# A hybrid diffusion step on one core: instruction order from the scheduler's timeline model

## The chip, the cores and the metric

The kernel runs on one core of a Trainium2 chip. A core has TensorE (PE, matmuls; PEld is its weight load), VectorE (DVE), ScalarE (ACT), GpSimd (POOL) and SyncE (SP), each with an instruction queue of its own that is worked off in order, and 16 DMA engines. The metric is the time of one execution on the device in microseconds (us), the median of several runs.

## The reference, cut to what matters

One inference step of a two-layer backbone of width 1024 over 640 tokens (128 context tokens, 512 latent tokens on a grid 64 wide). Layer 0 mixes tokens by a gated DeltaNet in both directions, layer 1 by neighbourhood attention; each mixer is followed by a gated ConvFFN of width 2816. Norms are RMSNorms with adaLN: shift, scale and gate are linear in SiLU of a conditioning vector (`modulation`).

```python
def modulation(cvec, w, b):
    m = jax.nn.silu(cvec) @ w + b
    return [t[:, None, :] for t in jnp.split(m, N_MOD, axis=-1)]
...
for l in range(DEPTH):
    mods, cmods = modulation(c, w_ada[l], b_ada[l]), modulation(c_ctx, ...)
    x = x + gate1 * mixer_l(rmsnorm(x) * (1 + scale1) + shift1)      # DeltaNet, then attention
    h = rmsnorm(x) * (1 + scale2) + shift2
    u = dwconv(h @ w_up)                 # two halves: value and gate
    x = x + gate2 * ((silu(u_gate) * u_value) @ w_down)
y = rmsnorm(x)
```

The block above is a condensed paraphrase below `modulation`. DeltaNet works in chunks of 64 tokens: for each head and direction a triangular inverse per chunk, and then a scan over the chunks in which the state S of one chunk enters the next.

## The kernel before, in words

Everything is held transposed: 128 channels on the partitions, the 640 tokens along the free axis, as eight tiles of the width. A product of f32 precision is made of three matmuls in a 32-bit reduced format: the weights are split into a high part `wh…` (a ScalarE cast, L373) and a low part `wl…` (a VectorE subtraction, L375), the activations into `hh` and `hl` (L346), and `pass3` (L385, L386, L387) issues high·high, high·low and low·high. So each weight tile has a DMA into a staging tile `wst…`, a cast on ScalarE and a subtraction on VectorE ahead of its matmuls.

Stages in the order of the program: adaLN products and the projections of the DeltaNet, its chunk work and scans (names `kk`, `p…` for chunk products, `sb`, `S`, `osb` in the scan, L915 to L972), its out-projection (`rgo`), the norm, FFN 0, the attention (heads in pairs `0` to `7`, names `s`, `t`, `no` on TensorE, `Ps`, `ptw` on VectorE; its out-projection is issued in an early part `rne` and a late part `rno`), the norm, FFN 1, the final norm.

An FFN takes 22 tiles of the hidden width. For each it makes two products, `duv` and `dug` (up-projection, value and gate halves, two halves of the tokens one after the other), in PSUM buffers of the pool `pd` (two; the pool `pa` has three smaller ones); a depthwise convolution of each follows (`conv`: ScalarE writes the middle tap at L437, VectorE adds the outer taps at L442 into `yv` and `yg`), then the gated product into `F`. The 22 tiles are worked in three groups; behind each, the down-projection `rdn` accumulates over the group's tiles of `F`, for eight output tiles (`rdn000` to `rdn007` for layer 0, group 0), and VectorE adds each to the residual stream `X` (L451).

The adaLN vectors that are needed only later are not made on TensorE but on VectorE: `ada_rows` loads rows of `w_ada` (256 KB tiles `adr…`) and reduces each with the conditioning vector, for both of its versions (`cb`, two reductions of 128 x 512 per tile, `adj` and `adr` as their throw-away outputs, L250). In FFN 0 `between` draws one or two steps of this generator behind each hidden tile, in FFN 1 another set in the same way.

The Python code doesn't give the order on the engines directly. The program is recorded by the tile framework, whose list scheduler then picks, engine by engine, which ready instruction is next. `behind` / `issue_after` (L320 to L328) forbid it to put certain instructions ahead of a given one, and `high_priority` raises some. Apart from these and from data dependences, the order follows from the scheduler's estimate of when an instruction would be ready and how long it takes.

## Time and profile before

| | |
|---|---|
| median of 3 runs | 1908.26 us (1902.61 to 1912.27) |
| profiled execution | 1907.08 us |
| its span, first to last instruction | 1905.1 us |
| granted TensorE clock, mean | 0.976 |
| busy: PE, PEld | 1808.2, 1717.7 us |
| busy: DVE, ACT, POOL | 1277.3, 724.3, 261.1 us |
| DMA | 194.15 MB, 102 GB/s mean |

All times of the trace are us from the start of the span of this one execution. The profile lists busy time by engine, the span in forty slices with the busy share of each engine in tenths, groups of equal instructions, waits with what ended them, and windows (a stretch, its length, then busy time and number of instructions of PE, PEld, DVE, ACT and POOL, the granted clock, the DMA share and GB/s). In the trace the DeltaNet's chunk work and scans run from about 100 to 560, FFN 0 from about 617 to 1084, the attention to about 1387, FFN 1 from about 1436 to the end.

### The profile page before, as it was taken

What the parts mean: (1) busy time and instruction counts of PE and PEld (TensorE: products, weight loads), DVE (VectorE), ACT (ScalarE), POOL (GpSimd) and SP (SyncE); (2) the same over time, 40 slices, a digit from 0 to 9 for tenths busy, and PEclk for the clock granted to TensorE, in tenths of its full rate; (3) what the DMA queues carried; (4) which work ended last, traced back from release to release, by engine and by line L of the source; (5) the groups of instructions that cost most, each with busy time, mean ns of one, the idle gap of its engine ahead of it and who ended that gap; (6) DMA issues with size and microseconds to landing.
All of it is one profiled execution on the core that took longest, in us unless ns stands there. A gap on an engine that the chain in (4) does not pass through costs nothing.

```text
span 1905.1 us, 34317 instructions
## 1 busy us (share of the span) xinstructions
PE 1808.2 (95%) x13587; PEld 1717.7 (90%) x13587; DVE 1277.3 (67%) x3100; ACT 724.3 (38%) x1456; POOL 261.1 (14%) x317
## 2 busy tenths in 40 slices
PE   6889899999879999999999999999999999999998
PEld 5878788887869999999999988888899999999998
DVE  6788658768666999855366689545679743653564
ACT  4553344343443342233144344444453421421443
POOL 1332123121202112110000211111131000000000
PEclk9989899999889999999999999999999999999999
DMA  7223123322222455542223254222233312222231
GB/s 293 74 81 106 39 103 114 93 64 80 74 97 93 143 169 160 160 159 67 82 83 111 71 164 153 76 74 71 68 122 117 117 56 78 88 71 75 88 90 56
DMA packets 102480, 194.15 MB, mean 102 GB/s; under 512 B 39496, under 2 KB 59034, under 8 KB 99560
## 3 DMA queue, kind: packets, MB, share of 16 engines
q1 hardware_dynamic: 94528, 165.50, 27.6%
q0 software_dynamic: 7248, 25.94, 4.3%
q8 instruction: 107, 1.75, 0.4%
q10 hardware_dynamic: 544, 0.52, 0.1%
q14 instruction: 53, 0.43, 0.1%
HBM read 183.09 MB, written 12.46 MB: 103 GB/s over the span
## 4 chain that ended last, share of the span: by engine, by line
PE 48%; DVE 4%; issue 2%; DMA 2%; ACT 1%; POOL 0%; DVEq 0%; POOLq 0%; ACTq 0%
PE duv L385 4%; PE duv L386 4%; PE dug L385 4%; PE dug L386 4%; PE duv L387 4%; PE dug L387 4%; PE rdn L385 4%; PE rdn L386 4%; PE rdn L387 4%; DMA bias<-cols 1%; PE dvn L385 1%; PE dvn L386 1%; PE dvn L387 1%; PE dqn L385 1%; PE no L1323 1%
## 5 line engine op out<-in xcount | busy, mean ns | idle before, releaser
L385 PE MATMUL duv<-hh,whuv 128*128 128x256 f32 (+1 forms) x704 | 215.8, 306 | 6.1 <-DVE yv L442 6.1
L385 PE MATMUL rdn<-F,whdn 128*128 128x384 f32 (+1 forms) x704 | 216.1, 307 | 3.1 <-DVE X L451 3.1
L386 PE MATMUL rdn<-F,whdn 128*128 128x384 f32 (+1 forms) x704 | 215.5, 306 | 0.0
L387 PE MATMUL rdn<-F,wldn 128*128 128x384 f32 (+1 forms) x704 | 215.5, 306 | 0.0
L385 PE MATMUL dug<-hh,whug 128*128 128x256 f32 (+1 forms) x704 | 215.2, 306 | 0.2 <-DVE yg L442 0.2
L386 PE MATMUL duv<-hl,whuv 128*128 128x256 f32 (+1 forms) x704 | 215.2, 306 | 0.0
L387 PE MATMUL duv<-hh,wluv 128*128 128x256 f32 (+1 forms) x704 | 215.2, 306 | 0.0
L386 PE MATMUL dug<-hl,whug 128*128 128x256 f32 (+1 forms) x704 | 215.2, 306 | 0.0
L387 PE MATMUL dug<-hh,wlug 128*128 128x256 f32 (+1 forms) x704 | 215.1, 306 | 0.0
L385 PEld LDWEIGHTS duv<-hh,whuv 128*128 128x128 f32 x704 | 132.2, 188 | 6.6 <-ACT whug L373 3.8
L385 PEld LDWEIGHTS rdn<-F,whdn 128*128 128x128 f32 x704 | 132.4, 188 | 3.8 <-issue 1.9
L451 DVE SCALAR_TENSOR_TENSOR X<-rdn,mods,X 128x128 f32<-128x128 f32 (+1 forms) x144 | 54.9, 433 | 116.0 <-PE rdn L387 115.9
L385 PEld LDWEIGHTS dug<-hh,whug 128*128 128x128 f32 x704 | 132.1, 188 | 0.3 <-issue 0.3
L387 PEld LDWEIGHTS duv<-hh,wluv 128*128 128x128 f32 x704 | 132.2, 188 | 0.1
L387 PEld LDWEIGHTS dug<-hh,wlug 128*128 128x128 f32 x704 | 132.2, 188 | 0.0
L386 PEld LDWEIGHTS duv<-hl,whuv 128*128 128x128 f32 x704 | 132.2, 188 | 0.0
L386 PEld LDWEIGHTS dug<-hl,whug 128*128 128x128 f32 x704 | 132.2, 188 | 0.0
L386 PEld LDWEIGHTS rdn<-F,whdn 128*128 128x128 f32 x704 | 132.1, 188 | 0.0
L387 PEld LDWEIGHTS rdn<-F,wldn 128*128 128x128 f32 x704 | 132.1, 188 | 0.0
L373 ACT CAST whdn<-wstdn 128x896 fp32r<-128x896 f32 (+1 forms) x48 | 47.0, 980 | 211.6 <-PE rdn L386 120.8
L373 ACT CAST whug<-wstug 128x1024 fp32r<-128x1024 f32 x44 | 46.2, 1050 | 139.2 <-PE dug L386 115.6
L375 DVE TENSOR_TENSOR wldn<-wstdn,whdn 128x896 fp32r<-128x896 f32 (+1 forms) x48 | 54.4, 1133 | 59.5 <-ACT whdn L373 59.5
(701 smaller groups left out, 4854.2 us busy)
## 6 DMA issues: line engine op xcount, KB each, us to landing
wstuv<-w_up SPq DMA_DIRECT2D x44, 512.0 KB, 3.5
wstug<-w_up SPq DMA_DIRECT2D x44, 512.0 KB, 3.6
adat<-w_ada SPq DMA_DIRECT2D x20, 1024.0 KB, 6.7
adr<-w_adar POOLq DMA_DIRECT2D x80, 256.0 KB, 3.2
wstdn<-w_dn SPq DMA_DIRECT2D x32, 448.0 KB, 3.4
wstdn<-w_dn SPq DMA_DIRECT2D x16, 512.0 KB, 3.6
adr<-w_adar SPq DMA_DIRECT2D x32, 256.0 KB, 2.8
wstqT<-w_gin SPq DMA_DIRECT2D x8, 512.0 KB, 3.6
```

Source lines behind the costliest of these rows:

```text
L373: nc.scalar.copy(wh[:, c], st[:, c])
L375: ins = eng.tensor_tensor(wl[:, c], st[:, c], wh[:, c].bitcast(F32), ALU.subtract).ins
L385: nc.tensor.matmul(out, a, mh, start=first, stop=False)
L386: nc.tensor.matmul(out, a, ml, start=False, stop=False)
L387: ins = nc.tensor.matmul(out, b, mh, start=False, stop=last).ins
L451: nc.vector.scalar_tensor_tensor(x, ps[:, base + c0 : base + c1], self.mod(l, gi, m, v), x, ALU.mult, ALU.add)
L1323: nc.tensor.matmul(out, vw[:n, cb, j, H[e]], pt[:n, 2 * e + j], start=(j == 0), stop=False, tile_position=(0, 64 * e))
```

## The change

The tile context is opened with `schedule_with_timeline_sim=True`. The list scheduler then keeps a timeline model of the engines and of the DMA queues while it picks instructions, in place of fixed figures per instruction. All instructions are recorded as before.

```diff
-    with tile.TileContext(nc) as tc, ExitStack() as ctx:
+    with tile.TileContext(nc, schedule_with_timeline_sim=True) as tc, ExitStack() as ctx:
         build(ctx, tc, aps)
```

The diff shows nothing of what moves, so here are three places of the two orders. Every engine's rows are the same set before and after, but for four more table loads on ScalarE.

FFN 0, VectorE, behind the low weights `wluv02` of the third hidden tile, before (numbers behind an underscore are buffers; `L250 ISA ad…` is a reduction, the shorter row behind it reads its sum out; `mods0`, `mods1` are the adaLN vectors of layer 0 and 1, `adh` a half sum):

```order
L375 TENSOR_TENSOR wluv02_7262<-wstuv020_7259,whuv02_7261 128x1024
L442 SCALAR_TENSOR_TENSOR yv01_7231<-duv01_7127,sm_61,yv01_7231 128x127
L442 SCALAR_TENSOR_TENSOR yv01_7231<-duv01_7127,sm_61,yv01_7231 128x511
L442 SCALAR_TENSOR_TENSOR yv01_7231<-duv01_7127,sm_61,yv01_7231 128x127
L442 SCALAR_TENSOR_TENSOR yv01_7231<-duv01_7127,sm_61,yv01_7231 128x511
L250 ISA adr0521_7392,mods0_77<-adr0521_7392,cb_6322,adh052_7399 128x512
L250 ISA mods0_77 128x1
L250 ISA adj0530_7538,adh053_7537<-adr0530_7397,cb_6322,sm_61 128x512
L250 ISA adh053_7537 128x1
L250 ISA adr0530_7397,adh053_7537<-adr0530_7397,cb_6322,sm_61 128x512
L250 ISA adh053_7537 128x1
L250 ISA adj0531_7543,mods0_77<-adr0531_7458,cb_6322,adh053_7537 128x512
```

After, from the same row on:

```order
L375 TENSOR_TENSOR wluv02_7262<-wstuv020_7259,whuv02_7261 128x1024
L442 SCALAR_TENSOR_TENSOR yv01_7231<-duv01_7127,sm_61,yv01_7231 128x127
L442 SCALAR_TENSOR_TENSOR yv01_7231<-duv01_7127,sm_61,yv01_7231 128x511
L250 ISA adr0570_7826,adh057_7900<-adr0570_7826,cb_6322,sm_61 128x512
L250 ISA adh057_7900 128x1
L250 ISA adj0571_7980,mods0_77<-adr0571_7832,cb_6322,adh057_7900 128x512
L250 ISA mods0_77 128x1
L442 SCALAR_TENSOR_TENSOR yv01_7231<-duv01_7127,sm_61,yv01_7231 128x127
L442 SCALAR_TENSOR_TENSOR yv01_7231<-duv01_7127,sm_61,yv01_7231 128x511
L250 ISA adr0571_7832,mods0_77<-adr0571_7832,cb_6322,adh057_7900 128x512
L250 ISA mods0_77 128x1
L250 ISA adj1000_7986,adh100_7985<-adr1000_7898,cb_6322,sm_61 128x512
```

Reductions now stand between the convs of `yv01`, where the convs were together; and they are those of `adr057` and `adr100`, four or five row tiles further on in the sequence than `adr052` and `adr053`, at the same place.

FFN 1, VectorE, the second half of the norm ahead of it: `nst121` is the mean square of the tokens, `nt12…` the normalized tiles, `hl_76` the low part of the activations. Before:

```order
L451 SCALAR_TENSOR_TENSOR X_6325<-rno17_15581,mods1_78,X_6325 128x256
L305 TENSOR_SCALAR nst121_15667<-nps121_15662 128x2
L250 ISA adj1500_16066,adh150_16065<-adr1500_15634,cb_6322,sm_61 128x512
L250 ISA adh150_16065 128x1
L250 ISA adr1500_15634,adh150_16065<-adr1500_15634,cb_6322,sm_61 128x512
L250 ISA adh150_16065 128x1
L341 SCALAR_TENSOR_TENSOR nt120384_15682<-X_6325,scg12_82,nrs121_15679 128x256
L341 SCALAR_TENSOR_TENSOR nt121384_15686<-X_6325,scg12_82,nrs121_15679 128x256
L341 SCALAR_TENSOR_TENSOR nt122384_15690<-X_6325,scg12_82,nrs121_15679 128x256
L346 SCALAR_TENSOR_TENSOR hl_76<-nt120384_15682,mods1_78,hh_75 128x256
```

After, from the second row behind `nst121` on:

```order
L250 ISA mods1_78 128x1
L250 ISA adj1510_16132,adh151_16131<-adr1510_16063,cb_6322,sm_61 128x512
L250 ISA adh151_16131 128x1
L250 ISA adr1510_16063,adh151_16131<-adr1510_16063,cb_6322,sm_61 128x512
L250 ISA adh151_16131 128x1
L250 ISA adj1511_16137,mods1_78<-adr1511_16069,cb_6322,adh151_16131 128x512
L250 ISA mods1_78 128x1
L250 ISA adr1511_16069,mods1_78<-adr1511_16069,cb_6322,adh151_16131 128x512
L250 ISA mods1_78 128x1
L250 ISA adj1520_16215,adh152_16214<-adr1520_16129,cb_6322,sm_61 128x512
L250 ISA adh152_16214 128x1
L341 SCALAR_TENSOR_TENSOR nt120384_15682<-X_6325,scg12_82,nrs121_15679 128x256
```

The first row shown reads out the reduction `adr1501`, which stands right behind `nst121`. So six reductions stand now between the mean square and `nt120384`, where two stood.

Attention, TensorE, the last pair of heads (7): `s73` are its last scores, `t72`, `tc72` the transposes of the third row group, `no7` the product with the values, `rne6` a tile of the early out-projection. Before:

```order
L1269 MATMUL s730_14981<-skn7_14612,sqn7_14439 128x192
L1269 MATMUL s731_14982<-skn7_14612,sqn7_14439 128x192
L1269 MATMUL s730_14981<-kc_11811,sqn7_14439 128x128
L1269 MATMUL s731_14982<-kc_11811,sqn7_14439 128x128
L1311 MATMUL t72_14998<-ident_63,Ps720_14916 124x128 x2
L1311 MATMUL t72_14998<-ident_63,Ps721_14918 124x128 x2
L385 MATMUL rne6_15018<-A0_11817,whne6_15014 128x384
L1314 MATMUL tc72_14999<-ident_63,Ps720_14916 128x128
L1314 MATMUL tc72_14999<-ident_63,Ps721_14918 128x128
L386 MATMUL rne6_15018<-A0_11817,whne6_15014 128x384
L387 MATMUL rne6_15018<-A0_11817,wlne6_15015 128x384
L385 MATMUL rne6_15018<-A1_12228,whne6_15014 128x384
```

After, from the same scores on:

```order
L1269 MATMUL s730_14981<-skn7_14612,sqn7_14439 128x192
L1269 MATMUL s730_14981<-kc_11811,sqn7_14439 128x128
L1269 MATMUL s731_14982<-skn7_14612,sqn7_14439 128x192
L1269 MATMUL s731_14982<-kc_11811,sqn7_14439 128x128
L1323 MATMUL no7_14816<-ptw71_14934,vw7_14766 64x128 x2
L1326 MATMUL no7_14816<-ptc71_14935,cv_11812 64x128
L1323 MATMUL no7_14816<-ptw71_14934,vw7_14766 64x128 x2
L1326 MATMUL no7_14816<-ptc71_14935,cv_11812 64x128
L1311 MATMUL t72_14998<-ident_63,Ps720_14916 124x128 x2
L1314 MATMUL tc72_14999<-ident_63,Ps720_14916 128x128
L1311 MATMUL t72_14998<-ident_63,Ps721_14918 124x128 x2
L1314 MATMUL tc72_14999<-ident_63,Ps721_14918 128x128
```

The transposes and products of head 7 follow one another; the matmuls of `rne6` that stood among them have been issued ahead, in the rows of head 6, and none stands between these and the late out-projection `rno`.

## Prediction, made before the changed kernel ran

> **What bounds the kernel now.** I read the page's busy totals first, then its forty slices, then a table of windows at the places where the two orders differ, then the waits and the timeline there.
>
> ```profile
> span 1905.1 us, 34317 instructions
> PE 1808.2 (95%) x13587; PEld 1717.7 (90%) x13587; DVE 1277.3 (67%) x3100; ACT 724.3 (38%) x1456; POOL 261.1 (14%) x317
> PE   6889899999879999999999999999999999999998
> DVE  6788658768666999855366689545679743653564
> PEclk9989899999889999999999999999999999999999
> ...
> core 0: us, PE busy (x) PEld busy (x) DVE busy (x) ACT busy (x) POOL busy (x), PEclk, DMA share, GB/s
> 617.00:735.00 118.00, 116.23 (x810) 115.75 (x809) 116.13 (x253) 45.90 (x58) 22.14 (x40) 1.00 0.51 157
> 735.00:800.00 65.00, 62.76 (x432) 62.30 (x430) 58.98 (x151) 9.03 (x10) 14.53 (x27) 1.00 0.51 161
> 1436.00:1462.00 26.00, 24.22 (x164) 23.87 (x164) 24.51 (x56) 11.79 (x17) 3.93 (x6) 1.00 0.34 105
> 100.00:560.00 460.00, 412.65 (x3729) 367.82 (x3727) 334.20 (x988) 187.93 (x552) 100.41 (x76) 0.94 0.28 83
> 1350.00:1392.00 42.00, 41.99 (x298) 37.37 (x296) 28.47 (x83) 19.09 (x48) 3.06 (x4) 1.00 0.29 90
> 1134.00:1194.00 60.00, 58.57 (x438) 51.79 (x439) 56.97 (x170) 27.39 (x66) 10.11 (x18) 1.00 0.48 149
> 1097.00:1134.00 37.00, 36.17 (x270) 32.46 (x269) 33.51 (x96) 16.13 (x36) 6.60 (x12) 1.00 0.54 169
> ```
>
> TensorE is busy 95% of the span, so any order can win at most 1905.1 − 1808.2 = 97 us, and loses wherever TensorE runs dry. Nearly half of that idle time, 460 − 412.65 = 47 us, lies in the DeltaNet's chunk work and scans (100 to 560), where the granted clock is also down to 0.94. Elsewhere TensorE has next to nothing to win. But at three places VectorE is as full as TensorE: 116.13 of 118 us at the start of FFN 0, 24.51 of 26 at the start of FFN 1, 56.97 of 60 in the second attention head. There an instruction put ahead on VectorE's queue delays everything behind it one for one.
>
> **The change, part by part.** No instruction is added or removed but four table loads of ScalarE (ACT has 1264 rows in place of 1260). The sum is therefore only of moves. From the two orders I counted, at each point where TensorE waits for VectorE, how many of the adaLN reductions (L250, two `adj` and two `adr` for a row tile and context) stand ahead of it. They are the movable mass: nobody needs them in their stage, they carry only modulations used later. One costs:
>
> ```profile
> 642.37 0.74 DVE L250 CUSTOM_DVE_ANT_0 adr<-adr,cb,adh 128x512 f32<-128x512 f32 x1
> ...
> 645.29 0.75 DVE L250 CUSTOM_DVE_ANT_0 adr<-adr,cb,adh 128x512 f32<-128x512 f32 x1
> ```
>
> From the first start to the last lie five reductions, four intervals: 2.92 / 4 = 0.73 us; the shortest pitch is 0.67, so I take 0.7 us each.
>
> *FFN 0, the largest term.* Ahead of the conv `yv02` the count goes from 21 to about 43, ahead of `wluv03` from 21 to 39, of `wluv05` from 39 to 61, of `wluv07` from 53 to 80, of `yv07` from 69 to 101, of the first residual add behind `rdn000` from 78 to 107, of `rdn004` from 100 to 128. From `rdn007` on both have done all 128. So nothing is saved: about 30 reductions that stood behind the up-projection, and beside the down-projection, now stand in front of convs. Who waits is seen in the waits of TensorE and at one place of its timeline:
>
> ```profile
> PE rdn L385 <- DVE X L451: 1.7, 1, 1.7
> PE duv L385 <- DVE yv L442: 1.7, 1, 1.7
> ...
> 631.13 0.41 PE L385 MATMUL duv<-hh,whuv 128*128 128x384 f32 x1 [1.68 <-DVE yv L442]
> ```
>
> The up-projection already stops once for a conv, since the conv frees its PSUM buffer; every conv that comes later holds the next `duv` longer. The most that stands extra is 32 at `yv07`: 32 × 0.7 = 22 us. From that goes VectorE's own idle time up to 735, 118 − 116.13 = 1.9 us, and one or two us that the PSUM buffers cover: **+18.5 us**. Least: if VectorE's lateness must first eat a lead of the size of the idle time of 735 to 800 (65 − 58.98 = 6 us) and of the two waits, 12; most: 22. It isn't regained in the down-projection: there TensorE is the bound (62.76 of 65 us), so a VectorE with less to do gives nothing back.
>
> *FFN 1.* The same move at the norm and the first convs. Ahead of `nst121` the count is 195 (before 192), of `nt120384` 201 (194), of the last `hl` 211 (195), of `wluv11` 215 (198), of `yv10` 217 (198), of `wluv12` 224 (203); equal again at `wlug14`.
>
> ```profile
> 1435.92 0.16 DVE L305 TENSOR_SCALAR nst<-nps 128x2 f32<-128x2 f32 x1 [1.85 <-PE nps L301]
> 1438.17 1.26 DVE L341 SCALAR_TENSOR_TENSOR nt<-X,scg,nrs 128x256 f32<-128x256 f32 x3 [0.58 <-PE nrs L314]
> 1447.67 1.23 DVE L375 TENSOR_TENSOR wluv<-wstuv,whuv 128x1024 fp32r<-128x1024 f32 x1 [0.29 <-ACT whuv L373]
> 1450.87 0.41 PE L385 MATMUL duv<-hh,whuv 128*128 128x384 f32 x1 [1.78 <-DVE yv L442]
> ```
>
> `duv` at 1450.87 starts as soon as the convs of `yv10` are done, after a wait of 1.78 us. 19 reductions more ahead of `yv10` are 19 × 0.7 = 13.3 us; VectorE's idle gaps in these rows can take 1.85 + 0.58 + 0.29 = 2.7 of it: **+11 us**, least 8 (five more hidden where the new order alternates `duv10` and `dug10`), most 14.
>
> *Attention.* Ahead of the norm's first tile `nt110384` the count goes from 128 to 134, at the first weights `wlvn0` it is 12 more, at the first residual-side tile `A0` 192 against 160; equal from head 2. Twelve are 8.4 us in front of the projections of head 0; VectorE was idle 37 − 33.51 = 3.5 us there, which leaves 5, and I take 7 − 3 = 4 with the six ahead of the norm. The 32 at `A0` (22 us) I take as nearly hidden: the new TensorE order runs projections a head ahead of the softmax, some 20 to 30 us of matmuls by my count of rows. The other loss is head 7, whose softmax in the kernel before is filled with the out-projection `rne`:
>
> ```profile
> L386 PE MATMUL rne<-A,whne 128*128 128x384 f32 x21 | 7.2, 345 | 0.0
> ...
> 1370.73 0.71 PE L1323 MATMUL no<-ptw,vw 92*64 92x128 f32 x6
> 1376.83 0.71 PE L1323 MATMUL no<-ptw,vw 124*64 124x128 f32 x6
> 1385.69 0.71 PE L1323 MATMUL no<-ptw,vw 96*64 96x128 f32 x6
> ```
>
> The first row counts one of three like groups between 1365 and 1387: some 62 `rne` matmuls, 10.7 us at a pitch of 0.17. In the new order none stands between the four row groups of head 7; they went into head 6. Between the first scores of head 7 and its last `no`, TensorE's own work falls to about 13 us, while the chain score, softmax, transpose, copy, `no`, with two groups in flight, took 15 us from the first `no` to the last even with fillers. I estimate the bare chain at 17 to 18 us from the scores on, so **+5** at the end, of 2 to 9. The whole stage: **+9**, least 2 (both hidden), most 20 (a third of the 22 us at `A0` shows besides).
>
> *DeltaNet, 100 to 560.* Here the new order moves much on TensorE and VectorE both, and with signs either way. The kernel before idles here (47 us), so a gain is possible.
>
> ```profile
> 100.00:150.00 50.00, 40.69 (x270) 37.55 (x272) 44.85 (x139) 21.31 (x41) 17.47 (x12) 0.86 0.26 79
> 168.00:206.00 38.00, 34.63 (x415) 29.76 (x414) 32.88 (x91) 13.26 (x43) 5.44 (x4) 0.91 0.23 70
> 541.44 0.34 DVE L966 SCALAR_TENSOR_TENSOR S<-S,egl,sb 128x128 f32<-128x128 f32 x1
> 545.30 0.80 DVE L966 SCALAR_TENSOR_TENSOR S<-S,egl,sb 128x128 f32<-128x128 f32 x2 [0.58 <-PE sb L964]
> 549.05 0.35 DVE L966 SCALAR_TENSOR_TENSOR S<-S,egl,sb 128x128 f32<-128x128 f32 x1 [0.46 <-PE sb L964]
> ```
>
> One scan step takes 3.8 us, from state to state (541.44, 545.30, 549.05), with hardly an independent matmul in it. By counting rows, the new order gives scans 2, 4 and 5 more filler than a step can hold (18 to 24 dense matmuls each) and scans 0, 3, 6 and 7 few; inverses stand 7 to 12 us of VectorE work earlier for heads 1 to 3, but from `p10` to the first output of head 0's scan VectorE has 37 us of work in the queue (29 before) against TensorE's 21 (31 before). That is +8 at one place, some −3 at the inverses: I take **+5**, from −15 (a third of the idle time recovered) to +20 (four thinly filled scans of eight steps that lose 0.6 us each).
>
> FFN bodies past these points have the same TensorE order; start and end I put at ±2. Sum: 18.5 + 11 + 9 + 5 = **+43.5 us** on the profiled execution's 1907.1 us (span 1905.1), which lies 1.2 us, 0.06%, under the median of the three runs, 1908.26: **1950 us**.
>
> One rule is weighed against the rows. The granted clock is 1.00 through FFN 0 even around the stop of 1.68 us, and 0.86 in the window from 100 to 150, where TensorE idles 9.3 us:
>
> ```profile
> 628.00:641.00 13.00, 11.32 (x78) 11.15 (x77) 12.63 (x27) 5.67 (x7) 1.61 (x3) 1.00 0.49 156
> ```
>
> The Trainium skill, "TensorE: Matmul & The Clock Gate", Part 1 (the HAM clock gate), says that an idle window of about 3.4 us halves the clock and that the same time of work brings it back. By that rule two gaps of 6 to 7 us at the norms would cost some 1.7 us more each, an estimate from that page, and the sum would be 1953; the rows agree so far that a short stop costs no clock.
>
> **The rivals.**
>
> *DeltaNet wins more than the rest loses* (the other side). Mechanism: in the scans the new interleaving closes the 47 us of idle time. It decides once the gain there exceeds the 38.5 us of the three other stages, that is over 80% of the idle time. For it: the clock at 0.94 would rise too, 6% of 412 is 25 us. Against: a step is a chain of 3.8 us across PE and DVE, and half the scans get less filler. Time then 1895 or less. Chance 4%. With the same gain about level, 1899 to 1917: 5%.
>
> *Mostly hidden.* Lateness of VectorE is taken up by TensorE's lead, since `pa` has three PSUM buffers and `pd` two. For: only two waits of 1.7 us each in FFN 0 before. Against: VectorE's 116.13 of 118 us, no lead grows while both are full. FFN 0 then costs 6, FFN 1 5, attention 2, DeltaNet 0: about 1920. Chance 11%.
>
> *Heavier.* The reductions, packed, run at the pace of their loads, and head 1's softmax and the thin scans show fully. The load of a tile of 256 KB takes:
>
> ```profile
> adr<-w_adar POOLq DMA_DIRECT2D x80, 256.0 KB, 3.2
> adr<-w_adar SPq DMA_DIRECT2D x32, 256.0 KB, 2.8
> ```
>
> With two or three tiles in flight that is 1.1 to 1.6 us a tile against 1.4 us for its two reductions; if issue and neighbours stretch it to 2.5, 32 tiles add up to 32 × 1.1 = 35 us at worst, and VectorE stands in order behind. 22 + 14 + 20 + 15 and a few us of loads: 1980. Chance 18%.
>
> *The change doesn't do what it says*: the orders differ on every engine, so this falls out.
>
> **How the numbers follow.** The main case, 1950 with its own range of 1932 to 1968, has the remaining 62%. Half a per cent is 9.5 us, about what a measurement of this kernel can tell from no change. Faster by more: 4%; within: 5%; slower: 91%. The range leaves out the first rival and most of the level case below, and the upper half of the heavy case above: 1918 to 1982.
>
> **What the trace after would show.** FFN 0: `rdn000` some 15 to 20 us later relative to the FFN's start, waits of `duv` and `dug` for `yv` and `yg` in several places of 1 to 4 us, and TensorE's share at 617 to 755 down to about 86%. FFN 1: one gap of some 10 us between the end of the out-projection and `duv11`. Attention: idle time among the four `no` of head 7, none among those of head 1. DeltaNet: a busy share in the scans about as before. The prediction is wrong if `duv` doesn't wait for `yv` although the order puts reductions between, or if the DeltaNet stage ends more than 15 us away from where it ended.

## The result: 4.6% slower

The changed kernel takes 1995.19 us (median of 4 runs, 1991.53 to 1997.94) against 1906.8 us (4 runs), a ratio of 1.0455 with a 95% interval of 1.0431 to 1.0480. The forecast was 1950, so the loss is 88 us where 43.5 were forecast, and outside the range. The profiled execution took 1991.53 us. Its page begins:

```profile
span 1989.4 us, 34340 instructions
PE 1843.5 (93%) x13587; PEld 1752.7 (88%) x13587; DVE 1276.5 (64%) x3100; ACT 725.8 (36%) x1460; POOL 260.0 (13%) x317
PE   6896899899879899999999899999997999999998
DVE  6677658777657999455455786555668553553564
PEclk9997899999889999999999999999998999999999
```

TensorE, VectorE and GpSimd have as many instructions as before, and VectorE is busy as long (1276.5 against 1277.3 us), but TensorE is busy 35 us longer with the same 13587 matmuls. That was in no term of the forecast: it only counted waits. Of the 84.3 us by which the span grew, the other 49 are idle time of TensorE; two questions stand: where this lies, and what makes equal matmuls take longer.

The starts of named tiles in the two traces cut the span into stages. (DeltaNet: to the end of its out-projection. FFN 0, 1 first: from the first `duv` to the first `rdn`, eight hidden tiles. Norm and head 0: from the first `dqn` to the first score `s`. Heads: to the last `no`.)

| stage, us | before | after | difference | forecast |
|---|---|---|---|---|
| DeltaNet and out-projection | 614.0 | 635.7 | +21.7 | +5 |
| FFN 0, first group | 113.9 | 128.9 | +15.0 | +18.5 |
| FFN 0, the rest | 352.2 | 352.0 | −0.2 | 0 |
| norm, projections of head 0 | 29.5 | 39.0 | +9.5 | +4 |
| attention heads | 277.5 | 301.7 | +24.2 | +5 |
| late out-projection | 46.5 | 43.0 | −3.5 | 0 |
| FFN 1, first group | 113.9 | 131.9 | +18.0 | +11 |
| FFN 1, the rest, to the last matmul | 351.3 | 350.9 | −0.4 | 0 |

FFN 0 came near its forecast. In the windows of the changed kernel (columns as before: busy time and number of PE, PEld, DVE, ACT, POOL, clock, DMA share, GB/s) its first group has VectorE full and TensorE starved. From its first `duv` to its first `rdn` VectorE is busy 127.7 us where it was 110.0, and its idle time fell from 3.9 to 1.2 us, which gives the 15.0:

```profile
635.00:765.00 130.00, 119.59 (x790) 117.16 (x789) 128.32 (x304) 43.78 (x57) 29.08 (x53) 0.97 0.51 164
```

FFN 1 shows the mechanism most plainly, in VectorE's timeline at the second half of the norm, and in TensorE's behind it:

```profile
1510.43 1.26 DVE L341 SCALAR_TENSOR_TENSOR nt<-X,scg,nrs 128x256 f32<-128x256 f32 x3
1511.60 0.75 DVE L250 CUSTOM_DVE_ANT_0 adr<-adr,cb,sm 128x512 f32<-128x512 f32 x1
1512.27 0.75 DVE L250 CUSTOM_DVE_ANT_0 adj<-adr,cb,adh 128x512 f32<-128x512 f32 x1
1512.95 1.27 DVE L346 SCALAR_TENSOR_TENSOR hl<-nt,mods,hh 128x256 fp32r<-128x256 f32 x3
...
1513.48 0.39 PE L386 MATMUL duv<-hl,whuv 128*128 128x256 f32 x1 [1.48 <-DVE hl L346]
1518.54 0.58 PE L386 MATMUL duv<-hl,whuv 128*128 128x256 f32 x1 [1.48 <-DVE hl L346]
1532.87 0.66 PE L385 MATMUL duv<-hh,whuv 128*128 128x384 f32 x1 [8.22 <-DVE yv L442]
```

Two reductions stand between each three norm tiles and their low parts. TensorE stops twice for 1.48 us for an `hl`, with a stop of 0.96 us for an `hh` between, then for 0.83 us, and in the end 8.22 us for the conv of `yv10`. Matmuls of 256 columns last 0.28 us ahead of the second stop of 1.48 us, and 0.58 (the first) and 0.41 us behind it, so the clock went down. The windows are the stretch up to the end of that stop, the one behind it, and the one behind the wait of 8.22 us:

```profile
1515.00:1518.30 3.30, 1.09 (x8) 0.69 (x6) 3.30 (x10) 1.31 (x3) 1.07 (x2) 1.00 0.28 83
1518.40:1521.70 3.30, 3.16 (x15) 3.17 (x16) 3.30 (x10) 0.66 (x2) 0.54 (x1) 0.50 0.31 89
1532.90:1538.80 5.90, 5.90 (x19) 5.90 (x20) 5.10 (x14) 2.74 (x3) 0.54 (x1) 0.50 0.32 115
```

So the short stops halved the clock too, once TensorE had worked only 1.09 of 3.30 us. Busy time times the missing half of the clock is 1.58 + 2.95 = 4.5 us of slow matmuls at this one seam, an estimate from these rows.

In the heads, both windows below hold the same matmuls but for 17 dense ones of the late out-projection, which stand inside the window only after (some 3 us; the stage behind got 3.5 us shorter). TensorE's busy time grew by 21.7 us, its idle time only by 2.6. By operation, the scores (line L1269, 256 records each) account for most of it, and those of line L1256, also on half of the rows, for another 3.4 us (3.4 before, 6.8 after):

```profile
1109.40:1386.80 277.40, 272.84 (x2068) 241.06 (x2067) 188.49 (x559) 119.18 (x299) 44.08 (x87) 1.00 0.31 96
1155.50:1457.20 301.70, 294.52 (x2085) 261.13 (x2084) 184.64 (x535) 116.00 (x300) 44.69 (x87) 0.99 0.27 83
...
1109.00:1387.00 278.00, 28.81 (x256) 21.81 (x256) 1.00 0.31 96
1155.00:1457.00 302.00, 44.45 (x256) 32.99 (x256) 0.99 0.27 84
```

The last two rows are the same stretches with L1269 alone: 28.81 and 44.45 us. TensorE's timeline shows why. Before, one row group of one head pair:

```profile
1253.82 0.58 PE L1269 MATMUL s<-skn,sqn 64*128 64x184 f32 x4
1254.24 0.39 PE L1269 MATMUL s<-kc,sqn 64*128 64x128 f32 x4
```

After, a row group of the same shape, in two pieces with nine projection matmuls between them:

```profile
1324.26 0.58 PE L1269 MATMUL s<-skn,sqn 64*128 64x184 f32 x2
1324.67 0.38 PE L1269 MATMUL s<-kc,sqn 64*128 64x128 f32 x2
...
1326.74 0.58 PE L1269 MATMUL s<-skn,sqn 64*128 64x184 f32 x2
1327.16 0.38 PE L1269 MATMUL s<-kc,sqn 64*128 64x128 f32 x2
```

Two records take as long as four. (A score instruction leaves two records, so a group, two heads by two operands, has eight.) The scores of one head use 64 of the array's 128 rows, and the code gives the two heads of a pair the two halves (`tile_position=(64 * e, 0)`). When the instructions of the two heads alternate, their records start some 7 ns apart and run side by side; when one head's stand alone, half the array is empty. Of the 32 groups of scores, 31 alternate before. After, one does in part, 15 have one head's directly behind the other's, and 16 are torn apart. Counted from start to start, the 32 groups take 26.7 us before and 40.8 us after; the 16 torn ones take 1.59 us each, where an alternating group takes 0.80, and are most of the loss.

In the DeltaNet TensorE's busy time is equal to 0.6 us, and all of the loss is waiting:

```profile
0.00:560.00 560.00, 490.93 (x4287) 436.94 (x4287) 401.28 (x1185) 236.69 (x651) 126.26 (x101) 0.94 0.32 99
0.00:579.00 579.00, 490.30 (x4284) 442.45 (x4285) 398.75 (x1185) 241.25 (x655) 124.12 (x101) 0.93 0.31 96
```

In the waits of that stretch (us in total, times, longest) the state product of the scans now waits more for ScalarE's `vn` and for `osb`, but less for the state S itself (5.2 us before, 0.5 after). No one wait carries the loss: of 19.7 us more, all waits of the state product `sb` make 3.3, and those for the blocks `W` and `Wx` that come by DMA 4.6; the rest is spread over some twenty rows. These are after, then before:

```profile
PE sb L964 <- ACT vn L931: 4.7, 11, 1.1
PE sb L925 <- ACT osb L957: 3.9, 6, 1.4
...
PE sb L964 <- ACT vn L931: 0.5, 1, 0.5
PE sb L925 <- ACT osb L957: 2.5, 2, 1.5
PE sb L950 <- DVE S L966: 5.2, 3, 2.9
```

### The profile page after: what moved, and what is told of

Its sections match the earlier page's. It is cut to its first block, busy times and chain, and to the rows that moved or that the text cites. A ratio compares the mean times of both kernels' runs of the same rounds, so it can differ in the third digit from the quotient of the medians.

```text
span 1989.4 us, 34340 instructions
## 1 busy us (share of the span) xinstructions
PE 1843.5 (93%) x13587; PEld 1752.7 (88%) x13587; DVE 1276.5 (64%) x3100; ACT 725.8 (36%) x1460; POOL 260.0 (13%) x317
## 4 chain that ended last, share of the span: by engine, by line
PE 57%; DVE 7%; issue 5%; DMA 2%; ACT 1%; POOL 1%; SPq 0%; POOLq 0%; DVEq 0%; ACTq 0%
PE rdn L385 5%; PE rdn L386 5%; PE rdn L387 5%; PE dug L385 4%; PE dug L386 4%; PE dug L387 4%; PE duv L385 4%; PE duv L386 4%; PE duv L387 4%; PE s L1269 2%; DVE adj L250 1%; PE dvn L385 1%; PE no L1323 1%; PE dvn L386 1%; DVE adr L250 1%
## 5 line engine op out<-in xcount | busy, mean ns | idle before, releaser
L375 DVE TENSOR_TENSOR wlug<-wstug,whug 128x1024 fp32r<-128x1024 f32 x42 | 51.3, 1222 | 69.1 <-ACT whug L373 69.0
```

Source lines behind the costliest of these rows:

```text
L375: ins = eng.tensor_tensor(wl[:, c], st[:, c], wh[:, c].bitcast(F32), ALU.subtract).ins
```

## The experiments

Two tools recur. `pin` puts each instruction of a list behind the one ahead of it on its engine; the lists are the orders of one engine, taken from a built kernel:

```diff
+def pin(tc, order):                       # order: lists of instruction numbers, packed
+    ins = {i.name: i for i in tc.nc.cur_bb.bb.instructions}
+    for names in unpacked(order):
+        for a, b in zip(names, names[1:]):
+            tc.add_manual_dep(ins[b], a, DependencyInfo(NoSync, DATA), reason="pin")
         build(ctx, tc, aps)
+        pin(tc, PINS)
```

The other holds the reductions in `ada_rows` behind the VectorE instruction that was recorded ahead of each:

```diff
-                nc.vector.tensor_tensor_reduce(
+                self.tc.keep_in_program_order(nc.vector.tensor_tensor_reduce(
                     junk, w, self.cb[:, v, h * n : h * n + n], 1.0, init, ALU.mult, ALU.add, out
-                )
+                ))
```

Stage lengths of all profiled runs, cut as above; the ratio is to the kernel before on the same chip. The same order of the DeltaNet (before, e6, e7, e8) gave 613.6 to 616.2, and FFN 1's first group in before, e6 and e7 113.9 to 115.8, so two or three us in a stage are scatter.

| | DeltaNet | FFN 0 first, rest | norm, head 0 | heads | FFN 1 first | median us | ratio (95%) |
|---|---|---|---|---|---|---|---|
| before | 614.0 | 113.9, 352.2 | 29.5 | 277.5 | 113.9 | 1906.8 | |
| after | 635.7 | 128.9, 352.0 | 39.0 | 301.7 | 131.9 | 1995.19 | 1.0455 (1.0431–1.0480) |
| e1 VectorE's order | 664.2 | 117.8, 357.3 | 32.3 | 318.2 | 121.0 | 2017.78 | 1.0587 (1.0553–1.0621) |
| e2 TensorE's order | 630.6 | 129.7, 353.3 | 34.0 | 283.8 | 124.2 | 1962.74 | 1.0295 (1.0271–1.0319) |
| e3 scores joined | 639.8 | 129.3, 350.7 | 41.2 | 290.9 | 130.7 | 1991.91 | 1.0449 (1.0407–1.0490) |
| e4 reductions held | 634.7 | 115.8, 360.2 | 30.3 | 318.5 | 123.2 | 1987.38 | 1.0426 (1.0402–1.0450) |
| e5 three repairs | 628.7 | 116.1, 361.0 | 27.5 | 282.4 | 123.0 | 1942.85 | 1.0181 (1.0162–1.0200) |
| e6 before, scores apart | 615.3 | 115.7, 354.6 | 28.5 | 280.6 | 115.5 | 1908.66 | 1.0003 (0.9981–1.0024) |
| e7 before, `no` alternates | 616.2 | 115.7, 352.8 | 29.1 | 272.4 | 115.8 | 1905.16 | 0.9962 (0.9944–0.9981) |
| e8 before, reductions held | 613.6 | 118.3, 365.2 | 49.5 | 276.3 | 122.4 | 1954.32 | 1.0241 (1.0223–1.0258) |
| e9 e5 and ScalarE, FFN 1 | 622.2 | 115.8, 359.7 | 27.0 | 282.9 | 116.2 | 1933.00 | 1.0112 (1.0085–1.0138) |
| e10 e9 and the queues | 618.9 | 115.8, 362.7 | 27.4 | 282.6 | 116.2 | 1927.29 | 1.0091 (1.0065–1.0117) |
| e11 two orders | 613.0 | 118.4, 355.9 | 30.3 | 275.9 | 115.5 | 1914.35 | 1.0016 (0.9990–1.0042) |

**e1: VectorE's order of before**, `pin` with one list.

> The changed kernel with VectorE's order alone put back to that of before, in all stages; the timeline model orders the other engines round it. Theory A (two separate causes: VectorE's order costs FFN 0, FFN 1 and the norm ahead of the attention, TensorE's order costs the DeltaNet and the attention heads, whose score matmuls of two heads no longer run side by side): FFN 0 -15 us, the norm and first head of the attention -10, FFN 1 -18 against the changed kernel, the scores as dear as in it, in all 1995 - 43 = 1952 us (1944 to 1962). Theory B (late reductions are the one cause, attention and DeltaNet are slow because VectorE is late): nearly everything comes back, 1915 us (1908 to 1925).

The stages in which the reductions matter came back as theory A said, at some two thirds of its size: FFN 0's first group −11 (the rest of FFN 0 +5), norm −7, FFN 1 −11 us against the changed kernel. But the total rose to 2018 us, which neither theory had: the model ordered TensorE anew round the given VectorE, the DeltaNet got 28 us longer, and the heads 16, with 24 groups of scores apart. VectorE's order put back alone isn't half a repair.

**e2: TensorE's order of before**, `pin` with one list.

> The changed kernel with TensorE's order alone put back to that of before; VectorE stays free and still has the reductions early in both FFNs. Theory A: DeltaNet -15 to -20 us, attention heads -18 to -25, FFN 0 and FFN 1 unchanged, in all 1995 - 40 = 1955 us (1945 to 1965). Theory B: FFNs unchanged, attention and DeltaNet at most -10 together, 1985 us or more.

The total is inside theory A's bounds, at their upper end. The heads came back by 18 us with the reductions still early, and FFN 0 stayed at 129.7: these two causes are separate. FFN 1's first group, which theory A left unchanged, came back by 7.7 us. The DeltaNet came back by 5, not 15 to 20; its state product still waits, and longer:

```profile
PE sb L964 <- ACT vn L931: 7.1, 10, 1.8
```

**e3: scores joined.** The list is TensorE's order of the changed kernel, in which the four score matmuls of a head pair are gathered at the place of the last, alternating; nothing else is moved:

```diff
-sA skn, sA kc, (others), sB skn, sB kc        # A and B: the two heads of a pair
+(others), sA skn, sB skn, sA kc, sB kc
```

> The changed kernel with TensorE's order unchanged but for one thing: the four score matmuls of a pair of heads (two heads by two operands) stand together and alternate between the heads, at the place of the last of them. Theory A: the scores' own time on TensorE falls from 40.8 + 6.2 us to some 30, total -12 to -18 us, 1980 us. Theory B: TensorE waits for VectorE anyway, 1995 us within 4.

The scores' time is back, and the heads are 10.8 us shorter; but TensorE's idle time there rose from 7.2 to 14.5 us, with new waits for the softmax's first step, since a joined group is as late as its later half. The window of the heads, L1269 alone, and the first wait:

```profile
1160.90:1451.80 290.90, 276.44 (x2068) 246.41 (x2067) 182.21 (x529) 115.08 (x295) 46.87 (x87) 0.99 0.28 85
1161.00:1452.00 291.00, 29.68 (x256) 22.29 (x256) 0.99 0.28 85
...
PE vt L1281 <- DVE sts L1194: 5.1, 4, 3.6
```

The total doesn't show the gain: its interval covers that of the changed kernel. In the profiled run the DeltaNet and the norm, whose TensorE order is the same, took 4 and 2 us more.

**e4: reductions held**, the second edit on the changed kernel.

> The changed kernel with the adaLN reductions alone held behind the VectorE instruction recorded ahead of each, so that they can't run ahead of the convs and norms (33 ahead of yv07 in place of 91, none ahead of the FFN 1 norm's tiles). Theory A: FFN 0 -15 us or a little more, norm and head 0 of the attention -10, FFN 1 -18 or a little more, DeltaNet and later heads unchanged: 1950 us (1940 to 1960). Theory B: 1915 to 1930 us.

FFN 0's first group −13 and the norm −9 us, near theory A; FFN 1 −9, half of what it had. VectorE is no longer full where TensorE starved:

```profile
634.00:751.00 117.00, 114.81 (x791) 114.08 (x790) 91.41 (x186) 44.95 (x57) 12.70 (x23) 1.00 0.38 116
```

The total gained 8 us, not 45. Two things ate the rest. The reductions now stand later in FFN 0, and hold one conv for 7.1 us there (+8 us in the rest of FFN 0). And the model, with other times ahead, ordered the heads otherwise: 22 groups apart, L1269 up to 50.68 us (in part by the clock, 0.95 there), the heads +17 us.

```profile
1141.00:1459.00 318.00, 50.68 (x256) 37.65 (x256) 0.95 0.29 88
PE duv L385 <- DVE yv L442: 7.4, 2, 7.1
```

**e5: three repairs**: the held reductions, and `pin` with TensorE's and VectorE's orders of before in the DeltaNet and TensorE's in the attention.

> The changed kernel with three repairs: in the DeltaNet the orders of TensorE and of VectorE together put back to those of before (e1 and e2 put back one each, and the stage stayed 50 and 17 us longer than before), in the attention TensorE's order alone, and the reductions held as in e4. Theory A (DeltaNet needs the two orders to fit each other; attention is TensorE's pairing; FFNs are the reductions): DeltaNet -18 us against the changed kernel, FFN 0 -8, norm -9, heads -20, FFN 1 -9, in all 1930 us (1918 to 1942). Theory B (the DeltaNet's loss is in ScalarE's and the queues' order): DeltaNet stays 15 us longer, 1947 us.

The norm (27.5), the heads (282.4) and FFN 1 (−9) came as in theory A; FFN 0 gave 4 us, not 8. The DeltaNet gave 7 us, not 18, as theory B had it, and the total lies between the two theories, just above the bounds of A.

**e6: scores torn apart in the kernel before.** TensorE's list of before, with 21 groups as one head's two, then the other's two, and 10 with three to six projection matmuls between.

> The kernel before, with TensorE's order changed in one thing: the score matmuls of 31 groups no longer alternate between the two heads of a pair; in 21 groups one head's two follow the other head's two, in 10 some three to six projection matmuls stand between them. From e1 and the changed kernel (8 and 15 groups in a row, 24 and 16 apart, 43.9 and 40.8 us of scores) a group in a row takes 1.1 us and one apart 1.46, against 0.83 when they alternate. Theory A: scores 39 us in place of 26.7, total +12 us, 1920 us (1914 to 1924). Theory B (the order among the scores costs nothing by itself, TensorE's matmuls take what they take): 1908 us within 4.

Not what theory A said. The scores took 36.69 in place of 28.81 us, not 12 more but 8: the 21 groups in a row cost no more than alternating ones. The second head's first record starts 13 ns behind the first head's, although two instructions stand ahead of it, and all run side by side: four records in the first row below, of both heads. (Start to start the scores sum up to 33.7 us: 0.81 in each group in a row, where 1.1 had been worked out, and 1.51 in each of the 11 with other matmuls between. In the changed kernel 4 of the 15 in a row overlap less or not at all; why is open.) So it is the matmuls between that cost. And half of what they did cost, TensorE had idle: idle time in the heads fell from 4.6 to 1.2 us, and the stage grew by 3.1. The total shows nothing.

```profile
1126.63 0.70 PE L1269 MATMUL s<-skn,sqn 64*128 64x248 f32 x4
1127.15 0.39 PE L1269 MATMUL s<-kc,sqn 64*128 64x128 f32 x4
...
1114.00:1394.60 280.60, 36.69 (x256) 27.98 (x256) 1.00 0.31 95
```

**e7: the products with the values alternate**, in the kernel before. The same idea on halves of the array's columns:

```diff
-            for e in range(2):
-                for j in range(2): matmul(O[H[e]], vw[.., j, H[e]], pt[:n, 2 * e + j], ..)
-                matmul(O[H[e]], cv[.. e], pc[:, e], ..)
+            for j in range(3):
+                for e in range(2):
+                    with net.behind(turn): turn = [matmul(O[H[e]], j-th operands of head e, ..).ins]
```

> The kernel before, with the products with the values (the six matmuls of each row group, three for each head of a pair) alternating between the heads, in place of three of one and three of the other. If matmuls on halves of the array's columns run side by side as scores on halves of its rows do, the 34.5 us of these matmuls fall to 25 or so: -6 to -10 us, 1900 us. If they overlap as well without it, 1908 us within 4.

The records' time fell from 29.64 (L1323) and 21.08 (L1326) to 28.09 us together, which stand as L1329 in the edited file; start to start the sum is 25.9 against 34.5. The heads are 5.1 us shorter, since 3.2 of the 8.6 us became idle time. The kernel is faster than before by 0.4% (0.9944 to 0.9981), and so beats both.

```profile
1109.00:1387.00 278.00, 29.64 (x256) 21.92 (x256) 1.00 0.31 96
1109.00:1387.00 278.00, 21.08 (x128) 15.82 (x128) 1.00 0.31 96
...
1113.00:1387.00 274.00, 28.09 (x384) 20.34 (x384) 1.00 0.32 97
```

**e8: reductions held in the kernel before.**

> The kernel before with the adaLN reductions held as in e4. Theory A (reductions ahead of convs and norm tiles cost TensorE time wherever VectorE is full, before too): VectorE falls from 110 to some 90 of 114 us in the first third of FFN 0, the waits for convs there and at the start of FFN 1 (1.7 and 1.8 us) go, but a late pack of reductions may hold a conv as in e4 (7 us): 1905 us (1898 to 1911). Theory B: no place where it tells, 1908 us within 4.

A miss, 49 us from the forecast: the reductions now collect at the end of FFN 0 and in front of the attention's norm, which went from 29.5 to 49.5 us, and more convs wait for them.

```profile
PE duv L385 <- DVE yv L442: 12.9, 10, 3.7
PE dqn L385 <- ACT hh L345: 8.2, 4, 4.0
...
1096.80:1146.30 49.50, 36.24 (x178) 31.46 (x178) 34.07 (x91) 19.87 (x41) 8.13 (x15) 0.72 0.27 89
```

The last row is the norm's stage, with the clock at 0.72 (0.94 before). TensorE's order moved too in this run, at the norm, in the heads and in FFN 1's first group, so not all of the 45 us is the reductions' place by itself. Still, the early reductions of the kernel before weren't waste; they fill VectorE's free time, and the changed kernel overdoes it.

**e9 and e10: ScalarE and the queues in the DeltaNet**, e5 with further lists: ScalarE's order of before in the DeltaNet and TensorE's in FFN 1 (e9), and GpSimd's and SP's in the DeltaNet too (e10).

> As e5, with ScalarE's order in the DeltaNet put back too (in e5 172 of its instructions there stood up to 7 places away from before, and SP's 93 up to 27 places), and TensorE's order in FFN 1 put back (in e5 the value and gate products of the first hidden tile alternate, and the next product waits 5 us and more for the conv). Theory C (scalar steps inside the scans, vn and osb, decide what is left of the DeltaNet): the stage falls from 628.7 to 617 us. Theory D (the order of the DMA issues on SP, which carry the inversion's blocks, decides): 627 us or so. FFN 1's first third falls from 123 to 115 us. In all 1943 - 12 - 8 = 1923 us by C, 1934 us by D.

> As e9, with all five queues of the DeltaNet in the order of before (SP and GpSimd too). By both theories the stage ends within 3 us of before's 614, and the total is 1921 us (1914 to 1928); what is left over before's 1908 is FFN 0, where the held reductions cost 7 to 9 us behind the first group. If the stage stays longer, the cause lies outside the five orders.

The DeltaNet went 635.7, 628.7 (e5), 622.2 (e9), 618.9 us (e10), against 613.6 to 616.2 in the four profiles of before's order. So theory C was half right: ScalarE's order, in which no instruction of e5 had moved by more than 7 places, is worth 6.5 us, as much as TensorE's and VectorE's together; the 3 us of the other queues are not clear of the scatter. TensorE's waits for the inversion, in e5 and e10, went with them (the changed kernel had only 5.0, so this wait is one of e5's own):

```profile
PE p L848 <- DVE W L869: 10.1, 6, 4.4
...
PE p L848 <- DVE W L869: 6.4, 6, 2.3
```

FFN 1's first group fell from 123.0 to 116.2 us by TensorE's order alone: of its 18 us, 9 are the reductions and 7 TensorE's order. What moved in that order is the alternation of `duv10` and `dug10`, whereby both are ready only together and the conv of the first starts late, and some sums of the norm with it; the alternation was not run alone. e9's total lies by theory D's, 1933 us; e10's is inside its bounds, 6 us over the middle, and its DeltaNet is 5 us over the 614 of the profile of before, where 3 were expected, which by the expectation would put a cause outside the five orders; e11, with the same five there, doesn't bear that out.

**e11: TensorE's and VectorE's orders of before throughout**, with the other three queues in the DeltaNet.

> The changed kernel with the orders of TensorE and VectorE of before throughout, and the other three queues of before in the DeltaNet alone; outside of it the timeline model still orders ScalarE, GpSimd and SP (nothing there moves by more than 4 places). If the orders are all there is to the change, 1909 us within 5, and FFN 0 behind its first group back from 363 to 352 us. If the model's mode costs something besides (other waits, other buffers), 1917 us or more.

1914.35 us, against 1911.94 for the kernel before on the same chip, a ratio of 1.0016 (0.9990 to 1.0042): no difference to before that these runs can tell. The DeltaNet is at 613.0 us, FFN 0 behind its first group at 355.9 (352 expected); with its first group FFN 0 is 4 us longer than in any of before, e6 and e7, which stays open. As far as these runs can tell, up to some 8 us, the orders are all there is to the change, and those of TensorE and VectorE, with the other queues in the DeltaNet, hold it.

## Why the prediction was wrong

The sign, and the stages that it named, were right. The size failed by 45 us, in three terms; and one of the signs that it gave for being wrong came true, the DeltaNet ending more than 15 us away.

*Attention, +9, at most 20.* Measured: +9.5 at the norm and head 0, +24.2 in the heads, −3.5 behind them. The step that failed is the one that counted only rows and waits on TensorE. It took the time of a matmul as given, while the pieces of the order shown ahead of the prediction had `s730`, `s730`, `s731`, `s731` where `s730`, `s731` alternated before (0.75 us before, 1.33 after, start to start). The dear groups, with other matmuls between, were not among the pieces shown. Losing the side-by-side execution of head pairs cost 15.6 us of TensorE's time at L1269 in the changed kernel, and joining them again gave back 10.8 us of the stage (e3). At the norm the cost was 9.5 us, not 4: what VectorE's idle time was to take off did not come off (that stage has 7.8 us of it before and 8.0 after), and the 7 in the prediction's "7 − 3" follows from none of its counts. e4 takes 9 of the 9.5 us away, so the reductions are the cause there. The loss at head 7 did not come: from the first to the last `no` it took 12.5 us (16.1 before).

*DeltaNet, +5, at most 20.* +21.7. The step that failed looked for the loss in the filler of the scans on TensorE, by counting rows; e2 shows that TensorE's order alone brings back 5 us. The loss is spread: e5, e9 and e10 put back 7, 6.5 and 3 us, with VectorE's order beside TensorE's, then ScalarE's, then the other queues'. ScalarE wasn't weighed at all.

*FFN 1, +11, at most 14.* +18: the reductions' part was 9 (e4), that of TensorE's order, with the alternating products, 7 (e9; 7.7 in e2). The prediction had named that alternation, and put it down as a possible gain.

*FFN 0, +18.5.* +15.0, inside its bounds of 12 and 22, and by the mechanism it gave: e4 takes 13 of it away by the reductions alone, and e2 none by TensorE's order. The counts at `yv07` were misread: in the traces 62 reductions stand ahead of it before and 91 after, 29 more and not 32.

*The clock.* By the rule of the Trainium skill weighed there ("TensorE: Matmul & The Clock Gate", Part 1) two gaps would have cost 1.7 us each. The trace agrees with the rule in kind (0.50 behind the wait of 8.22 us), but the rows above already give 4.5 us at one seam: TensorE worked 5.90 us at half clock behind that wait, and short stops that follow one another halved the clock too, which the prediction's sentence on short stops, drawn from a single one, had left out. The same shows in FFN 0 and at the norm:

```profile
651.40:658.10 6.70, 5.99 (x26) 5.70 (x27) 6.67 (x17) 2.61 (x4) 1.28 (x3) 0.50 0.40 122
1129.30:1136.00 6.70, 5.41 (x22) 4.82 (x23) 6.70 (x19) 2.61 (x6) 0.00 (x0) 0.50 0.25 78
```

With the two rows of FFN 1 that makes an estimated 10 us of slow matmuls in the three stages (before, the clock was 1.00 in two of them and 0.94 in the 29.5 us of the norm, under 2 us). Those in FFN 0 cost little, VectorE being full there. The clock belonged into the sum of FFN 1 and the norm, and the forecast's sum had nothing for it.

What stays open: the last 3 to 5 us of the DeltaNet in e10, which e11 doesn't have, and how much of the heads' loss would return if the scores were joined without being late; e3 shows 10.8 us of 24, e2, with all of TensorE's order, 18, and the other 6 have no cause shown.

## What to carry to other kernels

Where an order changes, compare not only what stands ahead of a waiting instruction but also which neighbours an instruction had: matmuls on halves of the array are only cheap next to their partner, and here the order from the timeline model of engines and queues tore them apart. Work that nobody waits for (here the reductions) has to be bounded from both sides: too early it stands in front of convs and norms on a full engine, too late it collects in front of the next stage (e8). And an order belongs to all engines together: putting back VectorE's list alone made the whole slower (e1), TensorE's alone gave back some 30 of 88 us (e2).

## What the hardware showed unexpectedly

Two score matmuls on the two halves of the array's rows start some 7 ns apart and run side by side, so that a group of eight records takes 0.80 us alternating, 0.81 us with one head's directly behind the other's (e6), and 1.5 to 1.6 us with matmuls on all rows between; for halves of the columns, alternating the heads saves a quarter of the start-to-start time (34.5 to 25.9 us, e7). A stop of TensorE need not be long to cost clock: repeated stops of 1.0 to 1.5 us (1.09 us of work in 3.30) brought it to 0.50 for some 3.3 us, as one of 8.22 us did for 5.9 us of work, and matmuls of 256 columns went from 0.28 to 0.41 us.
